# Even and odd channel groups of a state-space scan, put in the two halves of the partitions

## The chip, the cores and the metric

The kernel runs on one core of a Trainium2 chip. The metric is the device time of one execution in microseconds (us): the median of several executions. One more execution was recorded by the hardware profiler; its own time stands beside its span below.

## The reference, cut to what matters

The network is two blocks of two layers each on 256 positions of width 1024. Each layer of the first block has a mixer with three branches (a state-space scan, latent attention and a gated recurrence), a cross attention and a feed-forward part. The change is in the state-space branch, which runs once in each of the two layers of the first block. It has 32 groups of 16 channels, with 64 complex states each:

```python
def s5_mixer(u, lam_re, lam_im, b_re, b_im, c_re, c_im, d_skip, log_step, w_glu):
    uf = u.astype(jnp.float32).reshape(bsz, s, SSM_GROUPS, SSM_GROUP_CH)     # 32 groups of 16
    lam_bar = jnp.exp(lam * step)
    b_bar = ((lam_bar - 1.0) / lam)[..., None] * b_mat
    bu = jnp.einsum('bsgh,gph->bsgp', uf.astype(jnp.complex64), b_bar)
    # state[t] = lam_bar * state[t-1] + bu[t], along the 256 positions
    _, states = lax.associative_scan(combine, (a, bu), axis=1)
    y = jnp.real(jnp.einsum('bsgp,ghp->bsgh', states, c_mat)) + d_skip.astype(jnp.float32) * uf
    y = jax.nn.gelu(y.reshape(bsz, s, SSM_WIDTH)).astype(u.dtype)
    z_out, z_gate = jnp.split(y @ w_glu, 2, axis=-1)
    return z_out * jax.nn.sigmoid(z_gate)
```

## The kernel before, in words

All matrix products with weights go through `mm3`: a weight piece of 128x512 is read by DMA into `raw` (L375), split by ScalarE into a rounded part `whi` (L381) and by VectorE into a rest `wlo` (L382), and three matmuls (L387 to L389) add the products into a PSUM bank. These products fill most of the program on TensorE. PSUM has eight banks: three for `acc`, two for `tr` (transposes), two for `at` (attention scores and the recurrence's level products), and one, `sb`, that the state-space branch uses by itself.

The state-space branch takes four positions as one step of a scan, so 256 positions are 64 chunks of 4, and it works on 8 channel groups at a time. Such a set of 8 groups is called a unit here (`q` in the code); there are four units in each layer, eight in all. A unit has two parts.

`s5_build` makes what doesn't depend on the input. From the tables of the layer it makes `bT` (per group: 64 rows, which are 4 taps by 16 channels, against 128 states) on VectorE. Then, on TensorE and in this order in bank `sb`: the taps `kp` (L948, 8 matmuls with 64 columns of weights and 16 columns moving), from which VectorE makes `s5K` (L950), and four DMAs (L957) lay it out as the block-triangular `tz`, in the lower half of tile `B2`, after a memset by GpSimd (L955); and the turned `bL` (L963, 8 transposes in two runs of 4, each run evicted by ScalarE at L443 into `G0`). After that VectorE makes `cT` (L967 to L969) and the sine and cosine tables (L976 to L983).

`s5_apply` works on the input. Eight DMAs (L996) bring the 64 chunks into the upper half of `B2`; 8 transposes (L999) turn them, ScalarE evicts them as `U` (64 partitions x 8 groups x 64 chunks); 16 matmuls (L1006), each to one half of the output partitions, make the chunk inputs `vp` (128 x 512). VectorE multiplies by sine (L1011, two instructions of 64 partitions) and cosine (L1016), subtracts (L1017), scans (L1019), turns back (L1011, L1024, L1026) into `s5R`. Then TensorE makes the output: 8 matmuls of `U` with `tz` (L1031) and 8 of `s5R` with `cT` (L1033), each to one half of the output partitions, and after an eviction 8 matmuls with the identity (L1040), whose input and output lie in the same half. A `gelu` follows on ScalarE and VectorE.

TensorE takes these fp32 matmuls in two records each (8 matmuls are x16 in the trace); transposes are one record each. The text calls the states of one output half a column half of TensorE, and input partitions 0 to 63 or 64 to 127 a row half.

The order on each engine is made by a scheduler ahead of time from the program text, with priorities; an engine then works strictly in that order. In the mixer the units stand between other work: unit 0 is built while the first projections run (in layer 1: while the feed-forward part of layer 0 ends), unit 1 lies around the latent attention, units 2 and 3 around the recurrence (`hg_scores`, L774 to L810, in the two `at` banks). At the first unit of layer 0 the DMAs of `s5_build` are issued by ScalarE's queue, at the others by GpSimd's.

## Time and profile before

| | us |
|---|---|
| median of 3 executions | 1527.41 (1524.12 to 1531.72) |
| the profiled execution, its own time | 1526.91 |
| its span in the trace | 1525.1 |
| TensorE (PE) busy | 1445.4 (95%) |
| VectorE (DVE) busy | 1105.5 (72%) |
| ScalarE (ACT) busy | 822.1 (54%) |
| GpSimd (POOL) busy | 111.4 (7%) |

The span is that of the profiled execution; 1.8 us of its time lie outside. Busy times are those of the engine with at least one instruction in work. TensorE's matmuls overlap each other, so the duration of one is longer than the pace of a row of them; the pace is read here from the start of a run of matmuls to the start of what follows. Times of the rows are counted from the span's start.

### The profile page before, as it was taken

The page shows a single profiled execution, that of the slowest core. Times are in us where ns is not written, and L with a number is a line of the kernel's source. Part 1 is how long each engine was busy: PE and PEld are TensorE (multiplying, and loading weights), DVE is VectorE, ACT ScalarE, POOL GpSimd, SP SyncE. Part 2 cuts the span into 40 slices and gives each one's busy share as a digit, 9 for nine tenths or more (in the row PEclk, how much of TensorE's full clock was granted, in tenths as well). Part 3 has the DMA queues.
Part 4 walks back from the last instruction along what each step waited for, and adds up shares of the span by engine and source line. Part 5 has one row for each costly group of instructions (what it writes and reads, how often), then busy time and mean ns, then how long its engine had stood idle before and what let it go on. Part 6 is the DMA issues. An engine that isn't in the chain of part 4 may idle for free.

```text
span 1525.1 us, 27503 instructions
## 1 busy us (share of the span) xinstructions
PE 1445.4 (95%) x9604; PEld 1210.9 (79%) x9604; DVE 1105.5 (72%) x2250; ACT 822.1 (54%) x1769; POOL 111.4 (7%) x235
## 2 busy tenths in 40 slices
PE   6999999999999999989999999999999899989996
PEld 5788887878799987777877878799998676667774
DVE  7878788666598877668788675589875765676664
ACT  5475445546455555485545555555554455645563
POOL 1110012000100001101012000000000200000000
PEclk9999999999999999999999999999999999999998
DMA  5533435655489866533434675469877443444442
GB/s 187 181 121 111 140 104 170 189 181 172 133 281 291 272 192 184 166 106 106 135 104 134 211 231 162 135 216 315 273 208 240 118 150 104 141 138 159 132 126 76
DMA packets 143819, 258.97 MB, mean 170 GB/s; under 512 B 18016, under 2 KB 27072, under 8 KB 143680
## 3 DMA queue, kind: packets, MB, share of 16 engines
q1 hardware_dynamic: 133200, 239.30, 50.1%
q0 software_dynamic: 6288, 15.71, 3.4%
q10 hardware_dynamic: 4192, 2.22, 0.6%
q8 instruction: 75, 1.23, 0.3%
q14 instruction: 64, 0.52, 0.1%
HBM read 254.37 MB, written 1.08 MB: 167 GB/s over the span
## 4 chain that ended last, share of the span: by engine, by line
PE 76%; DVE 8%; ACT 6%; DMA 4%; issue 3%; POOL 2%; ACTq 0%; POOLq 0%; SPq 0%; DVEq 0%
PE acc L387 17%; PE acc L388 17%; PE acc L389 17%; PE tr L388 3%; PE tr L387 3%; PE tr L389 3%; PE tr L484 2%; PE at L800 2%; ACT whi L381 2%; DVE wlo L382 2%; PE at L537 2%; PE tr L565 2%; PE acc L592 1%; DMA raw<-in_wgu_dram 1%; PE tr L683 1%
## 5 line engine op out<-in xcount | busy, mean ns | idle before, releaser
L381 ACT CAST whi<-raw 128x512 fp32r<-128x512 f32 (+3 forms) x739 | 449.9, 614 | 381.4 <-PE acc L389 145.3
L382 DVE TENSOR_TENSOR wlo<-raw,whi 128x512 fp32r<-128x512 f32 (+3 forms) x739 | 495.3, 680 | 212.4 <-ACT whi L381 207.0
L388 PE MATMUL acc<-wlo,hTh 128*128 128x512 f32 (+3 forms) x588 | 232.6, 396 | 5.1 <-DVE wlo L382 4.9
L387 PE MATMUL acc<-whi,hTh 128*128 128x512 f32 (+3 forms) x588 | 233.7, 402 | 1.1 <-ACT whi L381 0.6
L389 PE MATMUL acc<-whi,hTl 128*128 128x512 f32 (+3 forms) x588 | 230.6, 393 | 0.0
L388 PEld LDWEIGHTS acc<-wlo,hTh 128*128 128x128 f32 x588 | 112.6, 192 | 25.3 <-DVE wlo L382 7.3
L387 PEld LDWEIGHTS acc<-whi,hTh 128*128 128x128 f32 x588 | 111.6, 191 | 25.8 <-issue 4.3
L387 PE MATMUL acc<-hTh,whi 128*128 128x256 f32 x448 | 128.5, 288 | 1.5 <-DVE H L739 1.4
L389 PEld LDWEIGHTS acc<-whi,hTl 128*128 128x128 f32 x588 | 112.6, 192 | 19.5
L388 PE MATMUL acc<-hTl,whi 128*128 128x256 f32 x448 | 127.9, 286 | 0.0
L389 PE MATMUL acc<-hTh,wlo 128*128 128x256 f32 x448 | 127.2, 284 | 0.0
L387 PE MATMUL acc<-whi,H 128*128 128x512 f32 (+1 forms) x222 | 88.5, 401 | 2.8 <-ACT whi L381 1.5
L387 PE MATMUL tr<-hTh,whi 128*128 128x256 f32 x320 | 90.6, 283 | 0.0
L388 PE MATMUL tr<-hTl,whi 128*128 128x256 f32 x320 | 90.6, 283 | 0.0
L389 PE MATMUL tr<-hTh,wlo 128*128 128x256 f32 x320 | 90.5, 283 | 0.0
L387 PEld LDWEIGHTS acc<-hTh,whi 128*128 128x128 f32 x448 | 85.8, 192 | 3.6 <-DVE H L739 1.9
L388 PE MATMUL acc<-wlo,H 128*128 128x512 f32 (+1 forms) x222 | 87.0, 392 | 0.7 <-DVE wlo L382 0.7
L389 PE MATMUL acc<-whi,H 128*128 128x512 f32 (+1 forms) x222 | 87.4, 394 | 0.0
L388 PEld LDWEIGHTS acc<-hTl,whi 128*128 128x128 f32 x448 | 85.8, 192 | 0.4
L389 PEld LDWEIGHTS acc<-hTh,wlo 128*128 128x128 f32 x448 | 85.7, 192 | 0.3 <-DVE wlo L382 0.2
L555 ACT ACTIVATE prob<-at,mx 128x256 f32<-128x256 f32 (+1 forms) x128 | 53.5, 428 | 24.7 <-DVE mx L549 17.9
L388 PEld LDWEIGHTS tr<-hTl,whi 128*128 128x128 f32 x320 | 61.4, 192 | 0.0
(529 smaller groups left out, 2930.8 us busy)
## 6 DMA issues: line engine op xcount, KB each, us to landing
raw<-in_win_dram SPq DMA_DIRECT2D x176, 256.0 KB, 3.1
raw<-in_wgu_dram SPq DMA_DIRECT2D x176, 256.0 KB, 4.5
raw<-in_wdn_dram SPq DMA_DIRECT2D x88, 256.0 KB, 3.0
raw<-in_wod_dram SPq DMA_DIRECT2D x64, 256.0 KB, 2.9
s5u<-in_wada_dram SPq DMA_DIRECT2D x48, 256.0 KB, 4.8
gate<-in_wada_dram SPq DMA_DIRECT2D x48, 256.0 KB, 5.0
raw<-in_wev_dram SPq DMA_DIRECT2D x40, 256.0 KB, 3.2
raw<-in_wglu_dram SPq DMA_DIRECT2D x32, 256.0 KB, 3.2
```

The costliest lines, as they stand in the source:

```text
L381: nc.scalar.copy(hi, raw)
L382: nc.vector.tensor_sub(lo, raw, hi)
L387: nc.tensor.matmul(ps, l[0], r[0], start=first, stop=False)
L388: nc.tensor.matmul(ps, l[0], r[1], start=False, stop=False)
L389: nc.tensor.matmul(ps, l[1], r[0], start=False, stop=last)
L484: nc.tensor.transpose(pt[:, j, :], src[:, (b + j) * P:(b + j + 1) * P], self.ident)
L537: nc.tensor.matmul(s[:, j, c], qT(h), kT(h)[:, c], start=not masks, stop=not masks or (j, k) == (hp - 1, nkt - 1))
L555: nc.scalar.activation(p[:, j, :], s[:, j, :], AF.Exp, bias=mx[:, j:j + 1], scale=scale, accum_out=den[:, hs[j]:hs[j] + 1])
L565: nc.tensor.transpose(pt[:, j * nkt + k, :], p[:, j, k * P:(k + 1) * P], self.ident)
L592: nc.tensor.matmul(o[a:a + 64, h, :], pts[:, j * nkt + k, a:a + 64], v(h, k), start=k == 0, stop=k == nkt - 1)
L683: self.nc.tensor.transpose(tp[:, j, :], src[:, j * w:(j + 1) * w], self.ident)
L800: nc.tensor.matmul(s[:, i, j, :], a, b, start=True, stop=True)
```

## The change: what it does

The groups of a unit are taken as 4 pairs of an even and an odd group. Everything that had 64 partitions and 8 groups (`kp`, `s5K`, `tz`, `U`) becomes 128 partitions and 4 groups, the even group in partitions 0 to 63 and the odd one in 64 to 127. The taps are made alternately in the two column halves; a pair of groups is turned by one transpose of 128 x 128, so there are 4 instead of 8, in one run with one eviction; the chunks are turned by matmuls with the identity instead of transposes, alternately in the column halves; the chunk inputs read row half 0 for even groups and row half 1 for odd ones, into two banks, `sb` and one of the two `at` banks; the taps' product with the input works in one row half and the same column half. `tz` moves from `B2` to the tile of `bL`, and the chunks' tile is taken in `s5_apply`. Weights and the skip are laid out to match outside the kernel's time. Per unit the DMAs of `tz` are 8 instead of 4, those of the skip 2 instead of 1.

```diff
-        dd = self.t([64, 8, 16], "s5dd")
-        self.q().dma_start(dd, self.A[f"ssmd{l}"][:, q * P:(q + 1) * P].partition_broadcast(64).rearrange("p o (g h) -> p (o g) h", g=8))
+        dd = self.t([P, 4, 16], "s5dd")
+        for f in range(2):
+            self.q().dma_start(dd[f * 64:f * 64 + 64], self.A[f"ssmd{l}"][:, q * P + f * 64:q * P + f * 64 + 64]
+                               .partition_broadcast(64).rearrange("p o (g h) -> p (o g) h", g=4))
...
-        kp = self.sb([64, 8, 16])
-        for g in range(8):
-            nc.tensor.matmul(kp[:, g, :], bT[:, g].rearrange("p t h -> p (t h)"), CX[:, g, :], start=True, stop=True)
-        K = self.t([64, 8, 16], "s5K")
+        kp = self.sb([P, 4, 16])
+        for g in range(4):
+            for f in range(2):
+                nc.tensor.matmul(kp[f * 64:f * 64 + 64, g, :], bT[:, 2 * g + f].rearrange("p t h -> p (t h)"), CX[:, 2 * g + f, :],
+                                 start=g == 0, stop=g == 3)
+        K = self.t([P, 4, 16], "s5K")
         nc.vector.tensor_add(K, kp, dd)
...
-        both = self.s("B2", [P, 4, 8, 16])
-        tz = both[0:64]
-        nc.gpsimd.memset(tz.rearrange("p t g h -> p (t g h)"), 0.0)
+        both = self.s("G0", [P, 1024])
+        bL = both[:, :512].rearrange("p (g n) -> p g n", g=4)
+        tz = both[:, 512:768].rearrange("p (t g h) -> p t g h", t=4, g=4)
+        nc.gpsimd.memset(both[:, 512:768], 0.0)
         for t in range(4):
-            self.q().dma_start(tz[0:16 * (t + 1), t], K[16 * (3 - t):64])
-        yield
-        bL = self.s("G0", [64, 8, P])
-        for hf in range(2):
-            tp = self.sb([64, 4, P])
-            for i in range(4):
-                nc.tensor.transpose(tp[:, i, :], bT[:, hf * 4 + i].rearrange("p t h -> p (t h)"), self.ident)
-            self.copy(bL[:, hf * 4:hf * 4 + 4, :], tp)
-            yield
+            for f in (0, 64):
+                self.q().dma_start(tz[f:f + 16 * (t + 1), t], K[f + 16 * (3 - t):f + 64])
+        yield
+        tp = self.sb([P, 4, P])
+        for g in range(4):
+            nc.tensor.transpose(tp[:, g, :], bT[:, 2 * g:2 * g + 2].rearrange("p f t h -> p (f t h)"), self.ident)
+        self.copy(bL, tp)
+        yield
...
-        uc = W["io"].rearrange("p t g h -> p t (g h)")
+        io = self.s("B2", [P, 4, 16, 8])[64:128]
...
-        up = self.sb([64, 8, 64])
-        for g in range(8):
-            nc.tensor.transpose(up[:, g, :], uc.rearrange("c t n -> c (t n)")[:, g:512:8], self.ident[64:, 64:])
-        U = self.s("B10", [64, 8, 64])
+        up = self.sb([P, 4, 64])
+        for g in range(4):
+            for f in range(2):
+                nc.tensor.matmul(up[f * 64:f * 64 + 64, g, :], io[:, :, :, 2 * g + f].rearrange("p t h -> p (t h)"),
+                                 self.ident[64:, 64:], start=g == 0, stop=g == 3)
+        U = self.s("B10", [P, 4, 64])
         self.copy(U, up)
-        vp = self.sb([P, 512])
-        for g in range(8):
-            for a in (0, 64):
-                nc.tensor.matmul(vp[a:a + 64, g * 64:(g + 1) * 64], W["bL"][:, g, a:a + 64], U[:, g, :], start=g == 0, stop=g == 7)
+        vp = [self.sb([P, 4, 64]), self.atb([P, 4, 64])]
+        for g in range(4):
+            for f in range(2):
+                for a in (0, 64):
+                    nc.tensor.matmul(vp[f][a:a + 64, g, :], W["bL"][f * 64:f * 64 + 64, g, a:a + 64],
+                                     U[f * 64:f * 64 + 64, g, :], start=g == 0, stop=g == 3)
...
-        w = crossed(vp)
-        V2 = self.s("B9", [P, 512])
-        nc.vector.tensor_mul(V2, vp, W["cs"])
+        w, V2 = self.s("B8", [P, 512]), self.s("B9", [P, 512])
+        for f, v in enumerate(vp):
+            crossed(par(w, f), v, par(W["sn"], f))
+            nc.vector.tensor_mul(par(V2, f), v, par(W["cs"], f))
...
-            nc.tensor.matmul(yp[f * 64:f * 64 + 64, g, :], U[:, f * 4 + g, :], W["tz"][:, :, f * 4 + g, :], start=g == 0, stop=False)
+            nc.tensor.matmul(yp[f * 64:f * 64 + 64, g, :], U[f * 64:f * 64 + 64, g, :], W["tz"][f * 64:f * 64 + 64, :, g, :], start=g == 0, stop=False)
```

The scheduler gives the changed program another order, in the units and between them. On TensorE, at unit 2 of layer 0, the kernel before stands so (`sb` and `at` are PSUM banks, `tm` the recurrence's table, `H` its input; line numbers are those of the kernel before):

```order
L999 MATMUL sb_2303<-cst_t,B_446_1866 64x64 x8
L774 MATMUL at_2386<-tm,H_211_847 128x512
L775 MATMUL at_2386<-tm,H_212_848 128x512
L774 MATMUL at_2390<-tm,H_211_847 128x384
L775 MATMUL at_2390<-tm,H_212_848 128x384
L1006 MATMUL sb_2314<-B_550_2312,G_447_1872 64x64 x16
L774 MATMUL at_2390<-tm,H_211_847 128x128
L775 MATMUL at_2390<-tm,H_212_848 128x128
L774 MATMUL at_2396<-tm,H_211_847 128x512
L775 MATMUL at_2396<-tm,H_212_848 128x512
L387 MATMUL acc_2269<-whi_2463,hTh_106 128x512
```

Of the changed kernel (its L1006, L1015 and L1043 are the chunk turns, the chunk inputs and the taps' product) the same place reads so, from the last of the four pairs of chunk-input rows on:

```order
L1015 MATMUL sb_2319<-B_549_2317,G_446_1873 64x64 x2
L1015 MATMUL at_2320<-B_549_2317,G_446_1873 64x64 x2
L774 MATMUL at_2395<-tm,H_209_845 128x512
L775 MATMUL at_2395<-tm,H_210_846 128x512
L387 MATMUL acc_2274<-whi_2473,hTh_106 128x512
L388 MATMUL acc_2274<-wlo_2474,hTh_106 128x512
L389 MATMUL acc_2274<-whi_2473,hTl_107 128x512
L387 MATMUL acc_2273<-whi_2491,hTh_106 128x512
L1043 MATMUL sb_2356<-G_446_1873,B_549_2317 64x64 x8
L774 MATMUL at_2399<-tm,H_209_845 128x384
L775 MATMUL at_2399<-tm,H_210_846 128x384
L774 MATMUL at_2399<-tm,H_209_845 128x128
```

The chunk inputs now stand ahead of the recurrence's first L774, with half of them in an `at` bank, and the taps' product between its first and second `at` tile.

On TensorE at unit 3 of layer 0, where the recurrence ends, the kernel before has the chunk inputs in two runs around a run of the recurrence's level products (L800), and all of them in `sb`:

```order
L1006 MATMUL sb_2731<-B_638_2729,G_594_2532 64x64 x9
L800 MATMUL at_2667<-E_617_2609 128x128 x4
L1006 MATMUL sb_2731<-B_638_2729,G_594_2532 64x64 x7
L822 MATMUL acc_2802<-H_424_1800,Q_530_2214 128x128 x2
L822 MATMUL acc_2829<-H_425_1802,Q_567_2421 128x128
L810 MATMUL at_2674<-E_617_2609,H_476_1982 128x128 x2
L824 MATMUL acc_2829<-H_424_1800,Q_573_2453 128x128
L822 MATMUL acc_2829<-H_425_1802,Q_567_2421 128x128
L824 MATMUL acc_2829<-H_424_1800,Q_573_2453 128x128
```

In the changed kernel the odd groups' chunk inputs stand behind the last `at` tiles of the recurrence (L800 and L810), and the taps' product is split around them:

```order
L800 MATMUL at_2678<-E_616_2620 128x128 x4
L389 MATMUL acc_2590<-whi_2707,oTl_352_1453 128x512
L387 MATMUL acc_2591<-whi_2707,oTh_436_1840 128x512
L388 MATMUL acc_2591<-wlo_2708,oTh_436_1840 128x512
L810 MATMUL at_2685<-E_616_2620,H_474_1986 128x128 x2
L389 MATMUL acc_2591<-whi_2707,oTl_437_1841 128x512
L1043 MATMUL sb_2776<-G_590_2524,B_637_2737 64x64 x3
L1015 MATMUL at_2740<-B_637_2737,G_590_2524 64x64 x8
L1043 MATMUL sb_2776<-G_590_2524,B_637_2737 64x64 x5
L822 MATMUL acc_2841<-H_425_1808,Q_567_2430 128x128
```

On ScalarE at the first unit of layer 0, where its queue issues the DMAs of `tz`, the kernel before has:

```order
L467 ACTIVATE junk_506,ssqb_505<-acc_343 128x256
L957 DMA B_95_462<-s5K_448 16x128
L957 DMA B_95_462<-s5K_448 32x128
L957 DMA B_95_462<-s5K_448 48x128
L957 DMA B_95_462<-s5K_448 64x128
L443 COPY G_99_480<-sb_481 64x512
```

and the changed kernel, with eight DMAs in four rows of two and one eviction of 128 x 512:

```order
L467 ACTIVATE junk_532,ssqb_531<-acc_344 128x256
L381 CAST whi_608<-raw_606 128x512
L964 DMA G_95_463<-s5K_449 16x64 x2
L964 DMA G_95_463<-s5K_449 32x64 x2
L964 DMA G_95_463<-s5K_449 48x64 x2
L964 DMA G_95_463<-s5K_449 64x64 x2
L443 COPY G_95_463<-sb_485 128x512
```

One weight piece's rounding (L381) has moved ahead of the DMAs, and the eviction behind them is twice as tall.

## Rows read from the trace of the kernel before

**Rows 1.** The page's first part: busy time of each engine.

```profile
PE 1445.4 (95%) x9604; PEld 1210.9 (79%) x9604; DVE 1105.5 (72%) x2250; ACT 822.1 (54%) x1769; POOL 111.4 (7%) x235
```

**Rows 2.** Windows: us, busy (x instructions) of PE, PEld, DVE, ACT, POOL; then PEclk.

```profile
30.00:60.00 30.00, 25.96 (x164) 20.37 (x163) 25.73 (x83) 11.34 (x27) 3.91 (x9) 0.89 0.54 166
...
790.00:830.00 40.00, 37.89 (x294) 31.00 (x289) 35.45 (x79) 20.27 (x55) 11.89 (x18) 0.96 0.35 110
```

**Rows 3.** Timeline of PE at unit 2 of layer 0: start, length, instruction.

```profile
192.36 0.66 PE L999 MATMUL sb<-cst_t,B 64*64 64x64 f32 x8
192.95 0.50 PE L774 MATMUL at<-tm,H 128*128 128x512 f32 x1
...
193.96 1.15 PE L1006 MATMUL sb<-B,G 64*64 64x64 f32 x32
195.03 0.33 PE L774 MATMUL at<-tm,H 128*128 128x128 f32 x1
...
202.63 0.69 PE L1033 MATMUL sb<-B,s5R 128*64 128x64 f32 x16
203.25 0.71 PE L800 MATMUL at<-E 128*128 128x128 f32 x4
...
204.36 0.68 PE L1040 MATMUL sb<-cst_t,B 64*64 64x64 f32 x16
204.97 0.50 PE L387 MATMUL acc<-whi,hTh 128*128 128x512 f32 x1
205.31 0.39 PE L388 MATMUL acc<-wlo,hTh 128*128 128x512 f32 x1
205.54 0.40 PE L389 MATMUL acc<-whi,hTl 128*128 128x512 f32 x1
...
208.89 1.08 PE L948 MATMUL sb<-B,B 128*64 128x16 f32 x16
209.90 0.51 PE L387 MATMUL acc<-whi,hTh 128*128 128x512 f32 x1
```

**Rows 4.** Timeline of PE at the first run of L963.

```profile
41.21 0.60 PE L963 MATMUL sb<-cst_t,B 128*64 128x128 f32 x4
41.56 0.48 PE L388 MATMUL acc<-wlo,hTh 128*128 128x512 f32 x1
```

**Rows 5.** Timeline of PE at unit 3 of layer 0.

```profile
226.45 0.79 PE L1006 MATMUL sb<-B,G 64*64 64x64 f32 x18
227.17 1.16 PE L800 MATMUL at<-E 128*128 128x128 f32 x8
228.26 0.68 PE L1006 MATMUL sb<-B,G 64*64 64x64 f32 x14
228.86 0.94 PE L822 MATMUL acc<-H,Q 128*128 128x128 f32 x6
...
239.85 0.69 PE L1033 MATMUL sb<-B,s5R 128*64 128x64 f32 x16 [1.53 <-DVE s5R L1026]
```

**Rows 6.** Groups of DVE by line and shape: busy, mean ns of one.

```profile
L1011 DVE TENSOR_TENSOR B<-sb,B 64x512 f32<-64x512 f32 x16 | 11.0, 688 | 4.1 <-PE sb L1006 3.9
...
L1016 DVE TENSOR_TENSOR B<-sb,B 128x512 f32<-128x512 f32 x8 | 5.5, 688 | 0.1
...
L1046 DVE TENSOR_TENSOR Q<-Q,sb 128x256 f32<-128x256 f32 x8 | 3.3, 412 | 0.0
```

**Rows 7.** Groups of ACT by line and shape.

```profile
L443 ACT COPY H<-tr 128x512 f32<-128x512 f32 x16 | 9.4, 590 | 8.9 <-PE tr L683 8.9
...
L443 ACT COPY B<-sb 64x512 f32<-64x512 f32 x8 | 4.7, 584 | 0.7 <-PE sb L999 0.7
...
L443 ACT COPY B<-sb 128x256 f32<-128x256 f32 x8 | 3.0, 372 | 10.2 <-PE sb L1033 6.6 <-DMA B<-s5u 3.6
```

**Rows 8.** Line L957 by itself: DMA issues of `tz`, ns min/median/max.

```profile
L957 POOL DMA_DIRECT2D B<-s5K x28: 501/511/545, 109.2 to 798.0; - x28
...
L957 ACTq DMA_DIRECT2D B<-s5K x4: 567/610/615, 40.9 to 42.8; - x4
```

More of the change, by code (lines that the diff above doesn't have):

```diff
@@ L62, in constants @@
     dl = np.zeros((P, 16))
-    dl[48:64, :] = np.eye(16)
+    dl[48:64, :] = dl[112:, :] = np.eye(16)
     c.add("delta", dl)
@@ L988, in s5_build @@
         flat = lambda v: v.rearrange("p g a b -> p (g a b)")
-        W[q] = dict(tz=tz, io=both[64:128], bL=bL, cT=cT, cs=flat(cs), sn=flat(sn), rho=rho.rearrange("p g c -> p (g c)"))
+        W[q] = dict(tz=tz, bL=bL, cT=cT, cs=flat(cs), sn=flat(sn), rho=rho.rearrange("p g c -> p (g c)"))
     def s5_apply(self, q, W, u, gT):
         nc = self.nc
-        uc = W["io"].rearrange("p t g h -> p t (g h)")
+        io = self.s("B2", [P, 4, 16, 8])[64:128]
+        uc = io.rearrange("p t h g -> p t (h g)")
         for t in range(NT):
@@ L1021, in s5_apply @@
         nc.gpsimd.memset(R[:, :, 0:1], 0.0)
-        w = crossed(X)
+        w = self.s("B8", [P, 512])
+        crossed(w, X, W["sn"])
         V2 = self.s("B9", [P, 512])
```

15 lines of the change are left out of this document (7 added, 8 removed).

## Prediction, on record before the changed kernel ran

> **What bounds the kernel now.** I read the page first. TensorE is busy for 1445.4 us of 1525.1, VectorE for 1105.5 and ScalarE for 822.1 [rows 1]: over the whole span TensorE is the bound, and work taken from it should come back as time, except where it waits. So the second view is windows around the units. From 30 to 60 us, where unit 0 of layer 0 is built, TensorE is busy for 25.96 us of 30 and VectorE for 25.73, at a granted clock of 0.89; from 790 to 830 us, where the recurrence of layer 1 ends with unit 3, TensorE for 37.89 of 40 and VectorE for 35.45 [rows 2]. In both VectorE is nearly as full as TensorE, so a TensorE saving there can turn into a wait. The third view is the timeline of TensorE at one quiet unit, since the pace of small matmuls can only be read from start to start [rows 3, 4]; the fourth is unit 3, where runs are split and TensorE waits 1.53 us for `s5R` [rows 5]. Last come the durations on VectorE and ScalarE and of the DMA issues [rows 6 to 8].
>
> **TensorE, step by step.** All per unit, and there are eight units.
>
> Taps. L948 makes 8 matmuls (16 records) in one column half; from its start to the start of the next row it takes 209.90 - 208.89 = 1.01 us. L1033, also 16 records over 128 input partitions but alternating the column halves, takes 203.25 - 202.63 = 0.62 [rows 3]. The changed taps have the form of L1033: -0.39, in eight units -3.1 us.
>
> Turns of `bL`. A run of 4 transposes takes 41.56 - 41.21 = 0.35 [rows 4]. One run of two disappears: -0.35, in eight units -2.8. The remaining ones are 128 x 128, and I give them the same pace (columns moving are the same 128).
>
> Chunk turns. Now 8 transposes take 192.95 - 192.36 = 0.59; 8 identity matmuls in alternating halves take 0.61 at L1040 (204.97 - 204.36) [rows 3]. Twice the records, the same time: +0.02, in all +0.2.
>
> Chunk inputs. 16 matmuls, already alternating column halves, take 195.03 - 193.96 = 1.07 [rows 3]. Now they alternate row halves too, so four quarters of TensorE are in use. No row of before shows four. The bounds are half (-0.53 a unit, -4.3) and, if two row halves broke the overlap of the column halves, the pace of L948, 32 records in 2.02 (+0.95, +7.6). I take no change, because L1040 is the nearest row: its two halves differ in row and column, and its 16 records in 0.61 are no faster than the 32 in 1.07.
>
> The Trainium skill, "TensorEngine Tiling (Array Packing)", section Key Properties, says that tiles operate independently and load weights and multiply in parallel; by that sentence the chunk inputs would take the half price and the sum would be lower by 4.3. The half price itself is a rival below, worked out from rows.
>
> Taps' product with the input. L1031 alternates column halves; it will alternate row and column, as L1040 does now. No change; the upper bound is the pace of L948 for its 16 records, +0.39 a unit, +3.1.
>
> L1040 writes from both row halves into one bank and takes 0.61 [rows 3], so a bank shared by row halves has no price in this trace. The Trainium skill, "TensorEngine Tiling (Array Packing)", section Restrictions and Gotchas, says that different row tiles cannot access one PSUM bank at the same time, which speaks against this step, since both row halves write `yp`; by it the sum would be higher by 3.1. The row doesn't bear that out.
>
> Split runs. Each run of small matmuls costs at its entry and its exit: at unit 3, L1006 in two runs takes (227.17 - 226.45) + (228.86 - 228.26) = 1.32 [rows 5] against 1.07 in one: +0.25. In the orders I count 58 runs of small matmuls before and 65 after (the turns of `bL` left out); about 4 of the 7 more don't adjoin another small run, so +1.0 (bounds 0 and 1.8).
>
> TensorE in all: -3.1 - 2.8 + 0.2 + 1.0 = -4.7. Of this the saving at unit 0 of layer 0, 0.39 + 0.35 = 0.74, I count as lost, because VectorE is as full as TensorE there [rows 2]; if it is not, it comes back (bound -0.7). That leaves -4.0.
>
> **VectorE and ScalarE.** The products with sine and cosine were 3 instructions, 688 ns each; they become 6 of 256 columns. A 256-column product with a PSUM operand takes 412 [rows 6], so 6 x 412 - 3 x 688 = +408 ns in the chain from `vp` to `s5R`. Ahead of it, the eviction of `U` falls from 584 to 372 [rows 7], -212. So the chain is 0.2 us longer. It is exposed where TensorE already waits for it, at unit 3 of layer 0 [rows 5], and I take unit 3 of layer 1, which has the same order, alike: +0.4. Elsewhere TensorE has other work in its order; as an upper bound VectorE's whole growth counts, 8 x 0.41 = 3.3 (the two operations on the skip have half the columns and can only shrink).
>
> ScalarE loses one eviction of 580 to 590 ns and 212 ns of another, about 0.8 a unit, 6.3 in all [rows 7]. ScalarE is busy for 54%, so I count nothing; it is a term of the faster rival. Its cost is at the first unit only: four more issues of `tz` at 610 ns and one of the skip, +3.1 us on ScalarE's queue, with the eviction of `bL` and the next roundings of weight pieces behind them [rows 8]. In the new order one rounding stands ahead of them, and ScalarE is busy for 11.34 us of those 30 [rows 2]: nothing, or +3.1 if TensorE runs out of weight pieces. On GpSimd five more issues of 511 ns a unit [rows 8] delay `tz`, which is needed only after the chunk inputs of that unit: nothing, while GpSimd's other work, the norms' scales, doesn't stand behind them.
>
> **The wait that is added.** Half of the chunk inputs now holds an `at` bank until VectorE has read it, behind the reads of `sb`: six instructions of 412, 2.5 us [rows 6]. There are two such banks. At unit 2 the order puts the recurrence's second `at` tile behind 2 + 3 + 1 matmuls of 512 columns and the taps' product. At 205.54 - 205.31 = 0.23 a matmul [rows 3] that is 6 x 0.23 + 0.61 = 2.0 us, so TensorE waits about 0.5 there, in two layers +1.0. At unit 3 the odd inputs stand behind the recurrence's last tiles, and the wait is the chain counted above. Around the attention (units 0 and 1) projections stand between: nothing. The upper bound is in the second rival.
>
> **Sum.** -4.0 + 0.4 + 1.0 = -2.6. The profiled execution took 1526.9 in its own time, so 1524.3. It lies 0.5 below the median of the three runs (1527.4); I leave the forecast at 1524.3. A difference of 0.5% is 7.6 us, about what a measurement of this kernel can tell from no change, so the forecast is "within 0.5%".
>
> **Rivals.** Faster: the four quarters do overlap. Then the chunk inputs cost 4.3 less, the 0.74 isn't lost, splits cost nothing and the bank's wait is filled: -3.1 - 2.8 + 0.2 - 4.3 = -10.0, which gives 1516.9; with a few waits of TensorE for ScalarE shortened, 1515. For it: TensorE is 95% busy. Against it: L1040's pace. Chance 0.24; it decides from -7.6.
>
> Slower, by one mechanism: the `at` bank. Scores and the recurrence's levels live on two banks, and if the held bank stops them wherever a unit lies beside them (units 1 to 3, both layers), 6 x 2.5 = 15 us of wait stand against the -4.0: +11.4 with the 0.4, which gives 1538.3. For it: VectorE works in order and is 89% full near unit 3 (35.45 of 40) [rows 2], so its six reads may come late. Against it: in most places TensorE's order has projections in between. It decides from a wait of 1.9 us in each of the six units (11.6 - 0.4 over 6). Chance 0.11.
>
> The change does nothing for the time: TensorE gets its 4.7 us back as waits for VectorE, whose work doesn't shrink. Then 1526.9. For it: VectorE's 25.73 of 30 and 35.45 of 40 [rows 2]. Against it: most of the span isn't like that. Chance 0.20. The forecast itself: 0.45, 1519.5 to 1530 by its own bounds (a half-clock stretch more or less included, since 0.89 over 30 us is 3.3 us).
>
> **How the numbers follow.** Faster 0.24 and slower 0.11 come from the first two rivals; the forecast and the case of no effect end within 0.5%: 0.65. The range takes in the first rival's end and reaches half way to the second's: 1515 to 1533.
>
> **What would show it.** In the profile after: taps at 0.62 a unit, one run of turns of 0.35, chunk turns at 0.61; chunk inputs at 1.07 (0.5 would be the faster rival, 2.0 would make me wrong upwards); TensorE's busy time lower by 4 to 6 us; six VectorE instructions of about 412 ns; waits of L774 and L775 for VectorE at unit 2 of about 0.5, and at unit 3 a wait for `s5R` of 1.5 to 2. I am wrong if the new order opens waits at places that I didn't cost, above all in the first 60 us, or if those for `at` sum to more than 5 us.

## The result, and the profile after

The changed kernel takes 1537.14 us (median of 13 executions, 1532.95 to 1541.67); the kernel before, on the same chip, 1530.37 (13 executions, 1524.12 to 1533.88). The ratio is 1.0058, with a 95% interval of 1.0045 to 1.0071: slower by 0.6%, where 1524.3 us and "within 0.5%" were forecast. (The ratio is the one on record for the two sets, and not the quotient of their medians, 1.0044; what is read from ratios and what from medians can differ by 2 us. As differences, -2.6 us was forecast and +6.8 came by the medians.) The profiled execution took 1535.45 us, with a span of 1533.7.

First the page's row of busy times, then windows (the columns are those of [rows 2]) of the changed kernel.

```profile
PE 1446.8 (94%) x9636; PEld 1210.8 (79%) x9636; DVE 1110.5 (72%) x2274; ACT 819.0 (53%) x1761; POOL 123.9 (8%) x270
```

```profile
30.00:60.00 30.00, 24.94 (x150) 18.89 (x151) 24.36 (x85) 10.90 (x26) 3.93 (x8) 0.77 0.48 140
...
226.00:250.00 24.00, 17.73 (x163) 14.85 (x162) 20.57 (x40) 10.45 (x35) 7.18 (x14) 0.86 0.33 108
```

The span grew by 8.6 us. TensorE's busy time, which was to fall by 4.7, rose by 1.4 [rows 1], so its idle time rose from 79.7 (1525.1 - 1445.4) to 86.9 us: +7.2. In that sum a gain is hidden, at the end of the program (below). Between 30 and 60 us its granted clock is 0.77 where it was 0.89 [rows 2]. Around unit 3 of layer 0, from 226 to 250 us, it is busy for 17.73 of 24 us at 0.86; in the kernel before that window reads:

```profile
226.00:250.00 24.00, 21.88 (x178) 17.62 (x177) 22.14 (x41) 14.51 (x43) 8.16 (x12) 1.00 0.46 144
```

**The end of the program.** Behind the last arithmetic, on ScalarE, the kernel before takes 1525.1 - 1516.4 = 8.7 us more, the changed kernel 1533.7 - 1529.9 = 3.8. ScalarE's last instruction, and the closing instructions of GpSimd's queue (ns min/median/max), before and after:

```profile
1515.71 0.72 ACT L1821 ACTIVATE xn<-xn,rsb 128x512 f32<-128x512 f32 x1 [1.10 <-POOL rsb L460]
L1847 POOLq DRAIN  x3: 46/98/9256, 1515.1 to 1524.9; - x3
...
1529.17 0.72 ACT L1833 ACTIVATE xn<-xn,rsb 128x512 f32<-128x512 f32 x1 [1.10 <-POOL rsb L460]
L1859 POOLq DRAIN  x3: 46/98/2232, 1528.5 to 1533.4; - x3
```

GpSimd's closing DRAIN lasts 9.26 us before, until 0.8 us from the end, and 2.23 after. The same end of 8.7 us stands in the traces of all four kernels with the instructions of before (before, and experiments 4, 8 and 12), that of 3.8 in all 13 with those of the change; in experiment 3 it is 4.3. So in the profiled executions 8.6 = 13.5 - 4.9: up to the last arithmetic the changed kernel loses 13.5 us, and 4.9 come back at the end, by a term that the prediction doesn't have. Why the DRAIN is shorter isn't shown.

**The small matmuls.** The timeline of TensorE in the changed kernel around unit 2 of layer 0, which answers to [rows 3]. Its lines: L952 taps, L968 turns of `bL`, L1006 chunk turns, L1015 chunk inputs, L1043 taps' product, L1045 the state's product.

```profile
195.94 1.18 PE L1006 MATMUL sb<-cst_t,B 64*64 64x64 f32 x16
197.04 0.50 PE L387 MATMUL acc<-whi,hTh 128*128 128x512 f32 x1
...
197.94 0.27 PE L1015 MATMUL sb<-B,G 64*64 64x64 f32 x2
197.95 0.27 PE L1015 MATMUL at<-B,G 64*64 64x64 f32 x2
...
198.41 0.23 PE L1015 MATMUL at<-B,G 64*64 64x64 f32 x2
198.56 0.50 PE L774 MATMUL at<-tm,H 128*128 128x512 f32 x1
...
200.17 0.88 PE L1043 MATMUL sb<-G,B 64*64 64x64 f32 x16
200.98 0.44 PE L774 MATMUL at<-tm,H 128*128 128x384 f32 x1
...
207.06 0.69 PE L1045 MATMUL sb<-B,s5R 128*64 128x64 f32 x16
207.68 0.94 PE L800 MATMUL at<-E 128*128 128x128 f32 x6
208.54 0.68 PE L1052 MATMUL sb<-cst_t,B 64*64 64x64 f32 x16
209.15 0.49 PE L800 MATMUL at<-E 128*128 128x128 f32 x2
...
213.70 0.65 PE L952 MATMUL sb<-B,B 128*64 128x16 f32 x16
214.28 0.50 PE L388 MATMUL acc<-wlo,hTh 128*128 128x512 f32 x1
...
215.74 0.60 PE L968 MATMUL sb<-cst_t,B 128*128 128x128 f32 x4
216.10 0.48 PE L387 MATMUL acc<-whi,hTh 128*128 128x512 f32 x1
```

From the start of a run to the start of what follows, the taps take 0.58 us (forecast 0.62) and the one run of turns 0.36 (0.35). The chunk inputs take 198.56 - 197.94 = 0.62 where they took 1.07 and were to stay there. The two banks' records start 0.01 apart and last 0.2 and more, so four quarters of TensorE are at work side by side. The chunk turns take 197.04 - 195.94 = 1.10, not 0.61, and the taps' product 0.81, not 0.61. Over the whole span, by the groups of TensorE by line (busy us; for L1015, whose two banks overlap, a window of that line alone):

| small matmuls of the state-space branch | before | after |
|---|---|---|
| taps | 9.1 | 6.1 |
| turns of `bL` | 10.0 | 5.4 |
| chunk turns | 5.9 | 12.8 |
| chunk inputs | 10.1 | 7.3 |
| taps' product | 6.0 | 7.5 |
| state's product and the last turn | 5.5 + 5.6 | 6.4 + 6.3 |
| sum | 52.2 | 51.8 |

So they gave 0.4 us and not 4.7 (a part of the rises is half clock, below). The same sum without the slow chunk turns comes with the last experiment.

**Where TensorE waits.** Its waits in the changed kernel (total us, times, longest):

```profile
PE sb L1045 <- DVE s5R L1038: 11.4, 2, 5.7
...
PE sb L952 <- DVE Q L1060: 3.6, 1, 3.6
```

In the kernel before the second of these didn't exist, and the first, one of whose two waits stands in [rows 5], was:

```profile
PE sb L1033 <- DVE s5R L1026: 3.1, 2, 1.5
```

Up to TensorE's last matmul (1511.7 and 1525.2 us) its idle time grew from 66.3 to 78.3 us, by 12.0; these two lines grew by 8.3 + 3.6 = 11.9, and what the other waits gained and lost cancels. The 11.4 us lie behind unit 3, half in each layer. The timeline of TensorE there in layer 0, which answers to [rows 5], and then that of VectorE:

```profile
236.41 0.71 PE L387 MATMUL acc<-whi,hTh 128*128 128x512 f32 x2
237.68 0.66 PE L484 MATMUL tr<-cst_t,w2a 128*128 128x128 f32 x4 [0.56 <-DVE w2a L832]
244.05 1.12 PE L1045 MATMUL sb<-B,s5R 128*64 128x64 f32 x16 [5.71 <-DVE s5R L1038]
245.10 0.90 PE L484 MATMUL tr<-cst_t,w2a 128*128 128x128 f32 x3
```

```profile
239.91 0.69 DVE L831 TENSOR_TENSOR w2a<-acc,hrsb 128x512 f32<-128x512 f32 x1 [1.15 <-POOL hrsb L460]
...
243.22 0.68 DVE L1038 TENSOR_TENSOR s5R<-B,B 128x512 f32<-128x512 f32 x1
243.82 0.69 DVE L832 TENSOR_TENSOR w2a<-w2a,H 128x512 f32<-128x512 f32 x1
244.42 3.09 DVE L382 TENSOR_TENSOR wlo<-raw,whi 128x512 fp32r<-128x512 f32 x5
```

Between the taps' product and the state's product TensorE has two projections left, and then nothing: the rests `wlo` that the next projections need are made by VectorE only behind `s5R` (five L382 from 244.42). The clock has then fallen: L1045 takes 245.10 - 244.05 = 1.05, against 0.62 at unit 2, the lower of the two levels (1.2 instead of 2.4 GHz), as the granted clock of the changed kernel shows (0.50):

```profile
244.00:247.00 3.00, 2.95 (x36) 2.42 (x37) 3.00 (x6) 0.37 (x1) 0.11 (x1) 0.50 0.20 60
```

In the kernel before, 16 projections stand in this place. Counted in the traces, the matmuls of `mm3` (512 or 256 columns, called projections here) between the last record of the taps' product and the state's product are:

| | unit 0 | 1 | 2 | 3 | layer 1: 0 | 1 | 2 | 3 |
|---|---|---|---|---|---|---|---|---|
| before | 0 | 11 | 11 | 16 | 30 | 19 | 11 | 16 |
| after | 62 | 26 | 10 | 2 | 38 | 24 | 10 | 2 |

At unit 0 of layer 0 the count says less: there the taps' product of the kernel before stands in three pieces, with 66 projections between the first and the last, and that of the changed kernel in two, with 3.

The 3.6 us are at the taps of unit 1 of layer 1, which now stand right behind the last turn of unit 0 and wait until the gelu has left bank `sb`:

```profile
697.57 0.68 PE L1052 MATMUL sb<-cst_t,B 64*64 64x64 f32 x16
701.84 1.04 PE L952 MATMUL sb<-B,B 128*64 128x16 f32 x16 [3.59 <-DVE Q L1060]
```

### The profile page after: what moved, and what is told of

It reads as the page before. It is cut to its first block, busy times and chain, and to the rows that moved or that the text cites. A ratio compares the mean times of both kernels' runs of the same rounds, so it can differ in the third digit from the quotient of the medians.

```text
span 1533.7 us, 27635 instructions
## 1 busy us (share of the span) xinstructions
PE 1446.8 (94%) x9636; PEld 1210.8 (79%) x9636; DVE 1110.5 (72%) x2274; ACT 819.0 (53%) x1761; POOL 123.9 (8%) x270
## 3 DMA queue, kind: packets, MB, share of 16 engines
q10 hardware_dynamic: 4496, 2.22, 0.5%
## 4 chain that ended last, share of the span: by engine, by line
PE 38%; DVE 5%; DMA 3%; ACT 2%; issue 2%; POOL 1%; POOLq 0%; ACTq 0%; SPq 0%; DVEq 0%
PE acc L387 8%; PE acc L388 8%; PE acc L389 8%; DVE wlo L382 1%; PE tr L388 1%; PE tr L387 1%; PE tr L389 1%; PE at L537 1%; PE tr L565 1%; PE acc L592 1%; PE tr L484 1%; ACT whi L381 1%; PE at L800 1%; DMA raw<-in_wgu_dram 1%; DMA raw<-in_wod_dram 1%
## 5 line engine op out<-in xcount | busy, mean ns | idle before, releaser
L381 ACT CAST whi<-raw 128x512 fp32r<-128x512 f32 (+3 forms) x739 | 450.4, 614 | 402.3 <-PE acc L389 146.5
L382 DVE TENSOR_TENSOR wlo<-raw,whi 128x512 fp32r<-128x512 f32 (+3 forms) x739 | 495.3, 680 | 226.3 <-ACT whi L381 220.0
L388 PE MATMUL acc<-wlo,hTh 128*128 128x512 f32 (+3 forms) x588 | 232.5, 396 | 5.0 <-DVE wlo L382 4.9
L388 PEld LDWEIGHTS acc<-wlo,hTh 128*128 128x128 f32 x588 | 112.4, 191 | 25.4 <-DVE wlo L382 6.6
L388 PE MATMUL acc<-hTl,whi 128*128 128x256 f32 x448 | 128.6, 287 | 0.0
L388 PE MATMUL tr<-hTl,whi 128*128 128x256 f32 x320 | 90.6, 283 | 0.0
L388 PEld LDWEIGHTS acc<-hTl,whi 128*128 128x128 f32 x448 | 87.1, 194 | 0.2
L388 PE MATMUL acc<-wlo,H 128*128 128x512 f32 (+1 forms) x222 | 86.4, 389 | 0.9 <-DVE wlo L382 0.9
L388 PEld LDWEIGHTS tr<-hTl,whi 128*128 128x128 f32 x320 | 61.4, 192 | 0.0
```

Source lines behind the costliest of these rows:

```text
L381: nc.scalar.copy(hi, raw)
L382: nc.vector.tensor_sub(lo, raw, hi)
L388: nc.tensor.matmul(ps, l[0], r[1], start=False, stop=False)
```

## The experiments

The theory after the result: the loss is the order. `s5_build` gives up control once less per unit (one run of turns, so one `yield` fewer), the scheduler writes another order, and TensorE runs dry at places where it had work before. The rivals: the held bank `at`; the small matmuls, above all the strided chunk turns; the split runs of VectorE. Ratios are to the kernel before on the same chip, with 95% intervals; medians of 6 to 13 executions. Places in the traces are read as "so much later than the kernel before", by matching the same matmuls in both; a single profiled execution lies up to 9 us from its kernel's median, so these tell where, not how much in all.

**1. The odd inputs in an accumulators' bank instead of `at`.**

```diff
-        vp = [self.sb([P, 4, 64]), self.atb([P, 4, 64])]
+        vp = [self.sb([P, 4, 64]), self.accb([P, 4, 64])]
```

> The changed kernel with the odd groups' chunk inputs in one of the three acc banks instead of an at bank. Theory 1 (the at bank holds the chain of unit 3 back): the two waits of TensorE for s5R, 11.4 us in the changed kernel, fall to about 3, as before, and the time falls by about 8 us, to within 2 us of the kernel before. Rival (the new order of the scheduler, not the bank, makes the loss): the waits stay above 8 us or appear elsewhere, and the time stays within 3 us of the changed kernel, 0.4% or more above the kernel before.

1540.53 us, ratio 1.0071 (1.0043 to 1.0099): not faster. The order moved again: 8 projections at unit 3 instead of 2, where the waits fall to 2.8 us each, but 97 instead of 62 at unit 0, and at 142 us this kernel is already 9 us late. So the bank didn't buy the time back; its own price isn't isolated by this, since the edit changes the order too.

**2. The chunks contiguous.** The columns of `u` and the chunks' tile are laid out so that a chunk turn reads its weights in one piece (its DMAs then move 64 bytes at a time).

```diff
-        io = self.s("B2", [P, 4, 16, 8])[64:128]
+        io = self.s("B2", [P, 8, 4, 16])[64:128]
...
-                nc.tensor.matmul(up[f * 64:f * 64 + 64, g, :], io[:, :, :, 2 * g + f].rearrange("p t h -> p (t h)"),
+                nc.tensor.matmul(up[f * 64:f * 64 + 64, g, :], io[:, 2 * g + f].rearrange("p t h -> p (t h)"),
```

> The changed kernel with the chunks laid out so that the weights of the chunk turns lie one after another instead of 32 bytes apart (the DMAs write 64-byte pieces). Theory (the stride makes the weight loads slow): the chunk turns fall from 60 ns a record to about 30, a unit's from 0.90 us to 0.47 between the first and the last start, and the time falls by 3 to 4 us against the changed kernel. Rival (the lower row half with alternating column halves is slow by itself): 60 ns stay and so does the time.

1538.61 us, 1.0070 (1.0046 to 1.0094). The pace is explained: weight loads of the changed kernel's chunk turns and of this one's, from the groups of PEld (the last number ahead of the second bar is the mean ns of one):

```profile
L1006 PEld LDWEIGHTS sb<-cst_t,B 64*64 64x64 f32 x128 | 10.3, 209 | 5.4 <-issue 3.8 <-ACT whi L381 0.7 <-PE acc L389 0.3
```

```profile
L1004 PEld LDWEIGHTS sb<-cst_t,B 64*64 64x64 f32 x128 | 6.1, 143 | 5.4 <-issue 3.8 <-ACT Q L486 0.7 <-PE acc L388 0.3
```

```profile
195.17 0.68 PE L1004 MATMUL sb<-cst_t,B 64*64 64x64 f32 x16
195.79 0.50 PE L386 MATMUL acc<-whi,hTh 128*128 128x512 f32 x1
```

0.62 instead of 1.10 us a unit. But the kernel isn't faster: the waits behind unit 3 are the same 11.4 us. The strided turns are a real cost of TensorE and not the cause of the loss. The edit has a price of its own that isn't separated from the gain: the packets on the DMA queue that carries the chunks grow from 4496 to 18832, and the median issue on ScalarE from 604 to 626 ns.

**3. The taps alone.** The kernel before with the taps in alternating column halves (the new layout of `kp`, `s5K` and the skip, eight DMAs for `tz`), nothing else.

```diff
-        kp = self.sb([64, 8, 16])
-        for g in range(8):
-            nc.tensor.matmul(kp[:, g, :], bT[:, g].rearrange("p t h -> p (t h)"), CX[:, g, :], start=True, stop=True)
+        kp = self.sb([P, 4, 16])
+        for g in range(4):
+            for f in range(2):
+                nc.tensor.matmul(kp[f * 64:f * 64 + 64, g, :], ...)
```

> The kernel before with the taps alone made in alternating column halves (and the DMAs of tz that this needs, eight instead of four a unit). If small matmuls saved on TensorE come back as time: taps at 0.6 us a unit instead of 1.0, time 3 us (0.2%) below the kernel before. Rival (each new order costs more than such a step saves): the taps are as fast, but the time is the same or up to 5 us above, with new waits of TensorE.

1524.50 us, 0.9971 (0.9951 to 0.9990), 4.4 us less than the kernel before by the ratio, with 15 projections at unit 3. That looks like the taps' saving, forecast at 3.1, but the trace doesn't bear it out: the end of this program is 4.3 us instead of 8.7, which is 4.4 by itself, and its last arithmetic ends at 1518.5 us, 2.1 later than before. TensorE is busy for 4.0 us less (1441.4), and idle for 6.2 us more up to its last matmul. So this run doesn't show that the taps' saving comes back as time.

**4. One step fewer in the kernel before.** The control: its instructions unchanged, one `yield` fewer a unit.

```diff
             self.copy(bL[:, hf * 4:hf * 4 + 4, :], tp)
-            yield
+        yield
```

> The kernel before with nothing changed but that the two runs of turns of bL are given to the scheduler in one step instead of two, as the changed kernel's one run is. It measures what a new order alone does. If order alone is small: within 2 us (0.13%) of the kernel before. Rival (the order alone makes the loss): 4 us or more above it, with new waits at unit 0, unit 1 or unit 3.

1542.50 us, 1.0087 (1.0057 to 1.0117): the order alone costs at least as much as the whole change, with the long end of 8.7 us kept. One place is the same: 4 projections at unit 3. TensorE in layer 0:

```profile
237.07 0.66 PE L484 MATMUL tr<-cst_t,w2a 128*128 128x128 f32 x4 [2.93 <-DVE w2a L832]
240.48 1.12 PE L1033 MATMUL sb<-B,s5R 128*64 128x64 f32 x16 [2.76 <-DVE s5R L1026]
```

2.93 + 2.76 = 5.69 us of wait, against 0.56 + 5.71 = 6.27 in the changed kernel. It isn't the only place: of the 16.6 us by which this profiled span is longer than that of the kernel before, about 4 come around unit 3 of layer 0 and 2 around that of layer 1; the rest is spread over the program.

**5. The missing step put back into the changed kernel.**

```diff
         self.copy(bL, tp)
         yield
+        yield
```

> The changed kernel with one more step: a second bare yield behind the copy of bL, so that the build of a unit has as many steps as in the kernel before; its instructions are those of the changed kernel. If the lost time came from the planner's order (one step fewer in the build, so that fewer projections stand behind the tail of unit 3), this one is at -3 to +1 us from the kernel before, and the wait for s5R at unit 3 is near 3 us again instead of 11.4 us for the line. If it came from the small matmuls themselves, the bank at or the split runs of VectorE, nothing changes: +7 to +11 us, as the changed kernel.

1530.96 us, 1.0013 (0.9992 to 1.0034): 0.45 of the 0.58 points are gone, with the change's instructions all in place. But the reason wasn't the one expected: the waits behind unit 3 are still 12.0 us, with 2 projections there. The time comes from the first 100 us, where this kernel is 1 to 3 us ahead of the kernel before and the changed one 2 to 4 behind; from 30 to 60 us the granted clock is 0.94 instead of 0.77. TensorE is busy for 1440.0 us instead of 1446.8 with the same instructions. So there is a second place.

**6. The same with contiguous chunks** (the edits of 5 and 2).

> The one before in this set, with the chunks laid out so that the weights of a chunk turn are read without stride. The turns of the chunks go from 1.11 to 0.65 us in each of 8 units. If both theories hold (the order for the loss, the stride for the pace), this is -4 to -8 us from the kernel before. If the order was not the cause, +6 to +10 us.

1534.50 us, 1.0038 (1.0017 to 1.0058). A miss: the chunk turns give up 0.5 us a unit, and the time doesn't fall.

**7. The same with the odd inputs in an accumulators' bank** (the edits of 5, 2 and 1).

> The second of this set, with both halves of the chunk inputs kept out of the bank at: the odd one goes to the accumulators' banks. If holding at costs by itself (the third theory), this is 2 to 5 us below the second; if it does not, within 2 us of it, either way.

1541.23 us, 1.0086 (1.0060 to 1.0111), with 163 projections at unit 0: worse, as in 1. Moving the bank costs more by the order than `at` can give.

**8. One step more in the kernel before.**

```diff
             yield
+        yield
         tmp = self.s("B9", [P, 8, 4, 16])
```

> The kernel before with one bare yield more behind the two turns of bL, that is one step more in the build instead of one fewer; same instructions. If the number of steps moves the time by the order alone, this differs from the kernel before by more than 0.2% in one direction or the other, with other waits for s5R, w2a and sb than there; if the loss of the experiment with one step fewer was an accident of joining two runs and two copies in one step, it is within 0.2%.

1530.64 us, 1.0008 (0.9984 to 1.0031): no difference that can be measured, with 14 projections at unit 3. So not every change of the number of steps costs; what counts is what the order then holds at the places where TensorE needs cover.

**9. Two lines of the mixer exchanged in the changed kernel.**

```diff
-        self.s5_apply(3, W[3], u, gT)
-        oH = self.hg_out(H)
+        oH = self.hg_out(H)
+        self.s5_apply(3, W[3], u, gT)
```

> The changed kernel with two lines of the mixer exchanged: the recurrence's output (hg_out) stands ahead of the last unit's s5_apply in the program text. In the order 16 projections then stand between the taps' product and the state's product of unit 3 in both layers, as in the kernel before, instead of 2 in the changed one; at the other units nothing moves. If the empty place behind unit 3 is the loss, the two waits of 5.7 us for s5R go to under 2 us each and the time falls by 6 to 10 us against the changed kernel: -2 to +3 us from the kernel before. If the loss sits in the small matmuls, the bank at or elsewhere in the order, it stays at +7 to +10 us.

1532.31 us, 1.0019 (0.9996 to 1.0042): 0.39 points below the changed kernel, with 16 projections at unit 3 and the other units as in the changed kernel. TensorE there:

```profile
242.16 0.66 PE L484 MATMUL tr<-cst_t,w2a 128*128 128x128 f32 x4 [0.93 <-DVE w2a L832]
245.57 0.69 PE L1045 MATMUL sb<-B,s5R 128*64 128x64 f32 x16 [2.76 <-DVE s5R L1038]
246.19 0.65 PE L388 MATMUL acc<-wlo,hTh 128*128 128x512 f32 x1
...
247.19 1.12 PE L1052 MATMUL sb<-cst_t,B 64*64 64x64 f32 x16
248.24 0.79 PE L388 MATMUL acc<-wlo,hTh 128*128 128x512 f32 x1
```

The wait for `s5R` halves (it was to go under 2 us) and the state's product runs at the full clock again (246.19 - 245.57 = 0.62); the clock falls right behind it, and the last turn takes 248.24 - 247.19 = 1.05. This kernel is still 3 to 5 us late from 65 to 190 us, as the changed one: that place isn't touched by the edit.

**10. The same with contiguous chunks** (the edits of 9 and 2).

> The one before in this set, with the chunks laid out so that the turns read their weights without stride. By the pace theory the chunk turns fall by 0.45 us a unit: 2 to 5 us below the first, so -2 to -6 us from the kernel before. If it equals the first, the time saved there falls into waits.

1532.60 us, 1.0029 (1.0005 to 1.0052): the second miss for the stride.

**11. The taps in a bank of the transposes as well** (the edits of 9 and 2, and this one).

```diff
-        kp = self.sb([P, 4, 16])
+        kp = self.trb([P, 4, 16])
```

> The second of this set, with the taps kp in a bank of the transposes (tr) instead of sb, so that the taps of unit 1 of layer 1 needn't wait until the gelu has left sb (3.6 us in the changed kernel). If that wait is a real loss: 2 to 4 us below the second of this set; if TensorE is given it back elsewhere, the same.

1527.95 us, 0.9997 (0.9978 to 1.0016): 4.65 us below 10 (1532.60 - 1527.95). The wait of 3.6 us is gone from the trace, so it looks like a real loss; the two intervals still overlap a little.

**12. The exchange in the kernel before** (the edit of 9).

> The kernel before with the same two lines exchanged, as a control: its unit 3 already has 16 projections behind the taps' product, 18 after the exchange. If the first of this set gains by filling the empty place, this one is within 2 us of the kernel before. If the exchange helps by itself, it is 3 us or more below it, and the gain of the first says nothing on the change.

1528.92 us, 1.0009 (0.9985 to 1.0034): the exchange gives nothing by itself, which fits that 9 gains by filling the empty place. It is a warning too: both waits for `s5R` at unit 3, 3.1 us in the kernel before, are gone here, and the waits of L388 for `wlo` grow from 5.5 to 8.9 us. A wait taken away can come back elsewhere.

**13. The four edits 5, 9, 2 and 11 together.**

> All four mends together: the missing step, hg_out ahead of the last s5_apply, the chunks without stride, the taps in tr. In the experiments with the exchange but without the step, TensorE ran 3 to 4.8 us late between 65 and 100 us, in the one with the step 1 to 3 us early. If that early place is a third loss of its own, this is 4 to 7 us below the experiment with everything but the step: -4 to -7 us from the kernel before. If it was swallowed later, -1 to +1 us.

1531.56 us, 1.0021 (1.0000 to 1.0042). A miss: with the step put back, the exchange leaves only 11 projections at unit 3, and there TensorE waits 2.9 us for `w2a` and 2.8 for `s5R` in a layer. What the first 100 us gave (2.5 us ahead at 153 us) goes there: at 243 us this kernel is 5.2 us late.

**14. The same with the chunks strided** (5, 9 and 11).

> The same with the chunks strided as in the changed kernel. The turns of the chunks cost 0.45 us a unit more. If that is paid at every unit: 2 to 4 us above the first of this set; the two earlier pairs showed no gain from the stride, so if the time falls into waits, within 1.5 us of it.

1530.49 us, 1.0016 (0.9997 to 1.0035), 1.1 us below 13: the third time that the stride's 0.45 us a unit doesn't show.

**15. Three steps more than 13.** Four bare `yield` behind the first instead of one.

> The first of this set with three steps more instead of one: in the order, at unit 0 of layer 0, 6 projections instead of 66 stand between the taps' product and the state's product (the kernel before: 0). If the output of unit 0 should come early there, 1 to 3 us below the first; if not, within 1.5 us or above.

1526.59 us, 0.9996 (0.9979 to 1.0013), 5.0 us below 13, where 1 to 3 were expected. At unit 0 of layer 0 it has 6 projections instead of 66; the clock of the first 60 us is 1.00 instead of 0.94, and at 153 us it is 5.7 us ahead of the kernel before. At unit 3 (10 projections) it loses that again.

**16. Each place mended by itself.** Three steps more at unit 0 alone; the exchange of 9, the chunks of 2, the taps' bank of 11.

```diff
         self.copy(bL, tp)
         yield
+        if q == 0:
+            yield
+            yield
+            yield
```

> Each place mended by the order that suits it: three steps more in the build of unit 0 alone (6 projections instead of 62 between the products of unit 0, as in the last experiment), the number of steps of the changed kernel at the other units together with hg_out ahead of the last s5_apply (16 projections at unit 3, instead of 10 in the last experiment), the chunks without stride, the taps in tr. If the three places add: unit 0 gives 3 to 6 us early as in the last experiment, unit 3 takes back 1 to 3 less than there, so -3 to -7 us from the kernel before. If they don't add, it is within 2 us of the kernel before, as the two experiments that it joins.

1519.80 us (9 executions, 1516.58 to 1525.47), 0.9951 (0.9931 to 0.9971): 0.5% faster than the kernel before and 1.1% faster than the changed one (1519.80 / 1537.14), the fastest of all. Against the kernel with everything but the three steps (11, 0.9997) it is 0.46 points faster, as much as 5 gained on the changed kernel, so the place at unit 0 adds to the others. Its profile has 6 projections at unit 0 and 16 at unit 3:

```profile
PE 1437.6 (94%) x9636; PEld 1203.1 (79%) x9636; DVE 1107.5 (73%) x2274; ACT 816.5 (54%) x1761; POOL 124.6 (8%) x270
...
PE sb L1047 <- DVE s5R L1040: 7.6, 3, 2.8
```

TensorE is busy for 7.8 us less than in the kernel before [rows 1], and the same seven groups of small matmuls, 52.2 us there, are 44.5 us here (5.6 taps, 5.9 turns, 5.9 chunk turns, 7.6 chunk inputs, 6.6 taps' product, 6.4 and 6.5): 7.7 less. But this isn't what the change is worth as time. In this profiled execution (1524.38 us, 4.6 above the median) TensorE is idle for 76.5 us up to its last matmul, 10.2 more than before, and that matmul ends 2.4 us later than before (1514.1 against 1511.7); the granted clock from 235 to 239 us, at unit 3, is 0.50. The span is 2.5 us shorter (1522.6 against 1525.1) by the end of the program, 3.8 us instead of 8.7. If the end is the same in the other executions, 4.9 of the 8.1 us between the medians are the end, and about 3 are what the new waits leave of TensorE's 7.8 (an estimate). The kernel before wasn't given three steps more at unit 0 or taps in `tr`, so what these would do without the change is open.

## Why the prediction was wrong, by its own steps

**Taps and turns: right.** 0.58 and 0.36 us a unit were measured for 0.62 and 0.35; as busy time over the span -3.0 us of the -3.1 for the taps, and -4.6 for the turns, where -2.8 had counted from start to start. That the taps' share comes back as time isn't shown: the gain of experiment 3 is the size of its shorter end.

**Chunk inputs: wrong, on the cheap side.** "I take no change, because L1040 is the nearest row" chose the wrong row: 1.07 became 0.62, near the lower bound of half. The Trainium skill, "TensorEngine Tiling (Array Packing)", section Key Properties, says that tiles load and multiply independently and in parallel; the trace agrees, with 32 records in 0.62 us in four quarters against 1.07 in two. L1040's 16 records in 0.61 had only two quarters in use, so its row could say nothing of four.

**Chunk turns: mis-sized.** +0.2 in all was forecast from L1040's pace; 12.8 - 5.9 = +6.9 us of busy time was measured. L1040 is the right shape with another layout of the weights: here they are read 32 bytes apart (209 ns a load against 143 in experiment 2). The row with the same layout stood beside it: the transposes L999 read the same chunks at the same stride, 8 records in 0.59, and 16 at that pace are 1.18, where 1.10 came. So "Twice the records, the same time" failed: with strided weights, twice the records took nearly twice the time, as if only one column half were in use (L948, 16 records in one half, takes 1.01). A strided load isn't slow in every case, since those of L999, in one column half, take 129 ns in the median:

```profile
L999 PEld LDWEIGHTS sb<-cst_t,B x64: 128/129/149, 47.0 to 809.0; 64*64 64x64 f32 x64
```

This ate the savings of TensorE. It was not given back by mending it alone (2, 6, 10, 14).

**Taps' product: mis-sized.** 0 was taken, with a bound of +0.39 a unit; +0.20 was measured at unit 2. The Trainium skill, "TensorEngine Tiling (Array Packing)", section Restrictions and Gotchas, has it that different row tiles can't use one PSUM bank at once. L1052, which also writes from both row halves into one bank, still takes 0.61, so the runs don't bear the rule out as the cause. Nor is the pace of L1043 lower: past its first three records a pair starts every 0.058 us, as at L1031 before. The 0.20 us lie between those first records, where TensorE's queue holds instructions that wait for semaphores; of these the taps' products have 38 in the eight units, against 24 before:

```profile
L1031 PEldq EVENT_SEMAPHORE  x24: 51/51/4715, 54.6 to 817.3; - x24
...
L1043 PEldq EVENT_SEMAPHORE  x38: 51/51/2178, 64.2 to 821.7; - x38
```

That they wait for the DMAs of `tz`, now eight instead of four, would fit and isn't tested.

**Split runs: not separated.** +1.0 was forecast for them, and no experiment isolates what the entry and exit of a run cost.

**The wait for `at`: it didn't come.** +1.0 was forecast at unit 2; L774 and L775 wait for nothing there. Whether holding `at` costs at unit 3 isn't separated from the order, since both edits that avoid it move the order (1, 7).

**The step that failed: the wait at unit 3.** "It is exposed where TensorE already waits for it, at unit 3 of layer 0 ..., and I take unit 3 of layer 1, ... alike: +0.4" sized the chain of VectorE and took the cover as unchanged. The chain isn't longer there: from the last chunk input to the end of `s5R` it takes 9.6 us at unit 3, where it took 10.8 (at unit 2 it is 8.3 for 7.4). The new order holds 2 projections behind the taps' product instead of 16, and the wait grew by 11.4 - 3.1 = 8.3 us, with a fall of the clock behind it. The new order could be read ahead of the run: a count of the projections between the two products at each unit would have shown 2 against 16. I counted runs that split, and not the cover of each wait. The prediction's own condition, that the new order opens waits at places that I didn't cost, above all in the first 60 us, is what happened; it had no rival and no chance of its own. That the order is the cause is shown, and not only argued: the control with one step fewer (4) loses 0.87% with the instructions and the end of the kernel before, and one bare `yield` (5) or two lines exchanged (9) take back 0.45 or 0.39 of the changed kernel's 0.58 points with its instructions in place. How much of the loss each place holds is less sure, since every edit moves the order at other places too.

**A term put at nothing: the end of the program.** The prediction counts up to the last matmul. The end fell from 8.7 to 3.8 us, so a part of what TensorE lost doesn't show in the time: without it the changed kernel would be slower by about 0.9%, and not 0.6 (8.9 us by the ratio, and 4.9 more; an estimate from the profiled executions).

**The rivals.** The bank's case (1538.3 us) gave nearly the measured time by luck, for another reason (as a difference it said +11.4, and +6.8 came); the waits for `at` at six units aren't in the trace. The faster case (-10.0, four quarters overlapping) was right as a mechanism. Experiment 16 lies 8.1 us below the kernel before in that set (1527.93 - 1519.80), but most of that is the shorter end, so it doesn't bear out the -10.0.

**Open.** How the scheduler comes to each order wasn't followed. In the first 100 us it is the granted clock that differs between the kernels (0.77 to 1.00 from 30 to 60 us), and in the changed kernel no single wait of TensorE from 28 to 100 us is longer than 2.1; which instruction makes the clock fall isn't shown. And why the faster chunk turns give nothing in four comparisons (2, 6, 10, 14) isn't settled: at the full clock 0.5 us a unit is 4 us, within the spread of such changes of order, and in all four the contiguous kernel has four times as many packets on the queue of the chunks' DMAs (18832 against 4496). What GpSimd's closing DRAIN waits for, 9.26 us before and 2.23 after, isn't shown.

## What to carry to other kernels

Where a scheduler writes the order, an edit that only merges two steps can cost more than the instructions it saves: count, ahead of the run, what the new order leaves behind each long chain, and compare it with the old count. A small change of TensorE work is to be tried in two or three orders (a step more, two calls exchanged), since its worth shows only in an order that keeps its cover. Compare the kernels up to the last matmul as well as by their whole span, since a shorter end can pass for a saving. And the nearest row for a matmul is one with the same quarters in use and the same stride of its weights, not one with the same shape alone.

## What the runs showed of the hardware that I had not expected

- Four 64 x 64 quarters at once: 32 fp32 records in 0.62 us, against 1.07 in two quarters.
- Weights read 32 bytes apart: a load of 64 x 64 fp32 takes 209 ns instead of 143, and 16 records 1.10 us instead of 0.62. The Trainium skill, "SBUF — State Buffer", section Door 1: The DMA port swizzle (why `[64,N]` ≈ `[32,N]`), says that accesses within 16 bytes (four fp32) are free and that each access crossing to a new line pays; the trace agrees for these loads (209 against 143 ns), and not for those of the transposes L999, which take 129 ns at the same stride.
- A wait of 5.7 us costs more than itself: behind it TensorE runs at the lower level (granted clock 0.50 from 244 to 247 us), 1.05 us for a run that takes 0.62.
- The end of a program can differ by 4.9 us between two kernels that end with the same arithmetic: GpSimd's closing DRAIN took 9.26 us in one and 2.23 in the other.
